# Moving operand addresses against the next stationary operand in a two-block transformer kernel

## The chip, the cores and the metric

One core of one Trainium2 chip runs the whole program. The metric is device time in microseconds from the first to the last instruction of the execution, with what lies around it; lower is better. Nothing is shared with other cores.

## The reference, cut to what matters

Two transformer blocks work on a sequence of 512 tokens of width 1024; the first of their three layers has a context of 256 tokens beside it. Between attention-like mixers stand six feed-forward networks, and these are most of the arithmetic:

```python
def swiglu(h, wi, wo):
    a, u = jnp.split(h @ wi, 2, axis=-1)      # 1024 -> 2 x 2816
    return (jax.nn.silu(a) * u) @ wo          # 2816 -> 1024
x = x + 0.5 * m[2] * swiglu(modulate(x, norm_g[l, 0], m[0], m[1]), ffn1_wi[l], ffn1_wo[l])
```

The modulation vectors `m` are products of a conditioning vector with large matrices, which the kernel reads while the feed-forward networks run.

## The kernel before, in words

Activations lie transposed: eight tiles `x0` to `x7` of 128 features by 512 tokens. Every float32 operand of a large product is split into a rounded part and a remainder, both of type float32r, so that `mm3` does three matmuls for one product: high weights by high activations (L182), high weights by low activations (L183), low weights by high activations (L184). The weights (`whi`, `wlo`, 128 columns of 512 bytes) are stationary, the activations (`hx`, `hc`, `g`, `mixr`, `mixa`: 512 or 256 columns) move through. TensorE therefore loads a new stationary operand ahead of every matmul, 16,678 times.

A feed-forward network (`ffn`, numbered 0 to 5) runs in four parts of 5, 5, 6 and 6 blocks of 128 hidden features. In each block `up` does 48 matmuls of the tiles `hx0` to `hx7` into `pau` (and 48 of `hc0` to `hc7` into `pc` in ffn 0, which has the context), `gate` makes a tile `g`, and at the end of a part `down` multiplies the `g` tiles into `py`, for eight output tiles `d`. The last four `d` of the last part, the tail, run by halves of 256 columns, so that the norm that follows can begin. A network that follows another begins with its first two blocks by halves too (256 columns), with weights that were fetched early into a pool `wb` by `prefetch` (two blocks' weights, or one block's in ffn 1 and 3). The mixers between use `fm` (weights stationary, activations moving) and `tm` (L668 to L670: activations stationary, 256 columns of weights moving).

Weights come by DMA on SyncE's queue into `wraw`, ScalarE makes `whi` (L177) and VectorE `wlo` (L178). The Tile framework orders the instructions by the waits that the tiles need; a tile may take over memory when the last reader of what lay there is done.

Where a tile lies follows from the order in which pools are opened and tiles first used. Pools on the left are stacked upward: constants, the `x` tiles, the weight pool `wp`, the temporaries `tp`, and above them the pools of the stage, among them `g0` to `g5` with the tiles `g`. Pools on the right are stacked downward from the end of the partition: `top` (a pad of 32 bytes), `hp0` with `hx0` to `hx7`, then `hc` and, when open, `wb`. A tile begins at a multiple of 32 bytes. The built program of the kernel before lists these first bytes of a partition:

| operand | first byte of one of its tiles | modulo 256 |
|---|---|---|
| `whi`, `wlo` in `wp` | 53056, 69440 | 64 |
| `hx`, also as `mixr` and `ph` | 196544 | 192 |
| `hc` | 180128 | 160 |
| `g` of ffn 0, tokens and context | 123264, 149888 | 128 |
| `g` of ffn 1, 3, 4, 5 | 102656 | 0 |
| `g` of ffn 2 | 124224 | 64 |
| `mixa` of the first, of the second mixer | 143424, 132864 | 64, 0 |
| weights in `wb` for ffn 1 to 5 and `w_in_2` | 163776 | 192 |
| weights in `wb` for `w_in` | 163712 | 128 |

The halves, the low parts, the blocks within a weight tile and the further tiles of a kind lie whole multiples of 256 bytes further on.

Of the kernel before, what the change touches and what calls it, by code (L numbers as in the profile page):

```python
# [8 lines left out]
F32 = mybir.dt.float32  # L9
F32R = mybir.dt.float32r  # L10
# [7 lines left out]
KC = 8  # L18
# [9 lines left out]
COLS = {}  # L28
NCST = 0
for _name, _w in [("b0", 72), ("b1", 72), ("b2", 72), ("ng0", 24), ("ng1", 24), ("fg", 8), ("pscale", 8),  # L30
                  ("gf1", 8), ("gmx", 8), ("gf2", 8), ("gfin", 8), ("gmh", 4), ("ba", 4), ("gbias", 1), ("glag", 1),
                  ("edge", 64),
                  ("gqk", 2)]:
    COLS[_name] = (NCST, NCST + _w)
    NCST += _w
CM = {n: 128 * i for i, n in enumerate(["ident", "glaf", "glab", "wprev", "wnext", "trif", "trib"])}
# [3 lines left out]
def program(ctx: ExitStack, tc: tile.TileContext, A, out):  # L40
    nc = tc.nc
    V, S, G, PE = nc.vector, nc.scalar, nc.gpsimd, nc.tensor
    const = ctx.enter_context(tc.tile_pool(name="const", bufs=1))
    act = ctx.enter_context(tc.tile_pool(name="act", bufs=1))
    wp = ctx.enter_context(tc.tile_pool(name="wp", bufs=2))
    tp = ctx.enter_context(tc.tile_pool(name="tp", bufs=2))
    pools = {}

    def opened(name, **kw):
        kw.setdefault("bufs", 1)  # L50
        g = tc.tile_pool(name=name, reuse_waits="tile", **kw)
        pools[name] = (g, g.__enter__())
        return pools[name][1]

    def opened_psum(name):
        return opened(name, bufs=2, space=bass.MemoryType.PSUM)

    def closed(*names):
        for name in names:
            pools.pop(name)[0].__exit__(None, None, None)  # L60
# [2 lines left out]
        for name in list(pools)[::-1]:  # L63
            closed(name)

    cst = const.tile([128, NCST], F32, name="cst")

    def C(name, i0=0, n=None):
        a, b = COLS[name]
        return cst[:, a + i0:(a + i0 + n) if n else b]  # L70
# [3 lines left out]
    ident = const.tile([128, 128], F32, name="ident")  # L74

    def load_constants():
        nc.sync.dma_start(cst, A["cst"])
        nc.sync.dma_start(ident, A["cmat"][:, CM["ident"]:CM["ident"] + 128])

    epst = const.tile([128, 4], F32, name="epst")  # L80
# [9 lines left out]
    def tmp(shape, dt=F32, name="tmp"):  # L90
        return tp.tile([128] + shape, dt, name=name, tag="t2k", bufs=5)
# [60 lines left out]
    def load_raw(src, shape):  # L152
        raw = wp.tile([128] + shape, F32, name="wraw", tag="raw", bufs=4)
        nc.sync.dma_start(raw, src)
        return raw

    def load_w(src, shape):
        return split_w(load_raw(src, shape), shape)

    ready = []  # L160

# [4 lines left out]

    def prefetched():
        if "wb" in pools:
            closed("wb")

    def take(src, shape):
        return ready.pop(0) if ready else load_w(src, shape)

    def split_w(raw, shape, pool=None, i=""):
        hi = (pool or wp).tile([128] + shape, F32R, name="whi", tag=f"whi{i}", bufs=1 if pool else 4)
        lo = (pool or wp).tile([128] + shape, F32R, name="wlo", tag=f"wlo{i}", bufs=1 if pool else 4)
        S.activation(hi, raw, AF.Copy)  # L177
        V.tensor_tensor(lo, raw, hi.bitcast(F32), OP.subtract)  # L178
        return hi, lo
# [6 lines left out]
    def split(src, hi, lo):  # L186
        a = S.activation(hi, src, AF.Copy)  # L187
        return a, V.tensor_tensor(lo, src, hi.bitcast(F32), OP.subtract)  # L188
# [78 lines left out]
    def new_h(s, pool):  # L267
        return [pool.tile([128, 2, s.n], F32R, name=f"h{s.name}{d}", tag=f"h{s.name}{d}", bufs=1) for d in range(KC)]
# [62 lines left out]
    def ffn(n, streams, hs, gate_m, steps, norm, early=None, g2=None, start=None, fused=False, nxt=(), mid=None, lag=False):  # L331
        X = streams[0]
        cx = streams[1] if len(streams) > 1 else None
        gp = opened(f"g{n}")
        ada_pool[0] = gp
        psum = opened_psum(f"pf{n}")
        gts = {}

# [14 lines left out]

        def gate(s, f, o):
            sl = tmp([s.n], name="sl")
            g = gp.tile([128, 2, s.n], F32R, name="g", tag=f"g{s.name}", bufs=6 if cx else 7)
            S.activation(sl, o[0], AF.Silu)  # L357
            V.tensor_tensor(sl, sl, o[1], OP.mult)  # L358
            gts[s.name, f] = g
            return split(sl, g[:, 0, :], g[:, 1, :])  # L360

        def wi(f):
            return [load_w(A[f"wi{n}"][f, p], [4, 2, 128]) for p in range(2)]

        def down(s, py, hi, lo, fs, c0, c1):
            for i, f in enumerate(fs):
                g = gts[s.name, f]
                mm3(py[:, :c1 - c0], hi[:, i, :], lo[:, i, :], g[:, 0, c0:c1], g[:, 1, c0:c1], i == 0, i == len(fs) - 1)

        def resid(s, d, py, c0, c1, last):  # L370
            V.scalar_tensor_tensor(s.x[d][:, c0:c1], py[:, :c1 - c0], s.gate[:, d:d + 1], s.x[d][:, c0:c1],  # L371
                                   op0=OP.mult, op1=OP.add)
            if last:
                s.square(d, c0, c1, g2)

        for pi, (f0, f1) in enumerate(PARTS):
            nk = f1 - f0
# [3 lines left out]
            if pi == 0:  # L381
                o = {f: bank2(X) for f in (0, 1)}
                if start:
                    o[2] = [psum.tile([128, T], F32, name="pau", tag="y") for _ in range(2)]
                    w, raw = {f: [] for f in range(3)}, {}
# [15 lines left out]
                else:  # L401
                    w = {f: [take(A[f"wi{n}"][f, p], [4, 2, 128]) for p in range(2)] for f in (0, 1)}
# [7 lines left out]
                    for f in (0, 1):  # L410
                        up(X, w[f], o[f], range(KC), *X.halves[1])
                    todo = todo[2:]
                    prefetched()
                for f in o:
                    last_gate = gate(X, f, o[f])
# [21 lines left out]
            def downs(ss, ds):  # L437
                for d in ds:
                    hi, lo = load_w(A[f"wo{n}_{pi}"][d], [nk, 128])
                    for s in ss:  # L440
                        py = psum.tile([128, 512], F32, name="py", tag="y")
                        down(s, py, hi, lo, fs, 0, s.n)
                        resid(s, d, py, 0, s.n, last)
# [17 lines left out]
            nt = 4 if last else 0  # L461
# [4 lines left out]
                if last and nxt[d:d + 1]:  # L466
                    prefetch(nxt[d:d + 1])
            if last:
                w = [load_w(A[f"wo{n}_{pi}"][KC - nt + i], [nk, 128]) for i in range(nt)]
                half = {s.name: norm(s) for s in streams}  # L470
                tail = [(s, c0, c1) for s in streams[::-1] for c0, c1 in s.halves]
                for s, c0, c1 in tail:
                    for i in range(nt):
                        py = psum.tile([128, 512], F32, name="py", tag="y")
                        down(s, py, w[i][0], w[i][1], fs, c0, c1)
                        resid(s, KC - nt + i, py, c0, c1, True)
                    if lag and c0:
                        late.apply()
                    late = Late(s, c0, c1, fused, half[s.name])
                    if (s, c0) != tail[-1][:2]:  # L480
                        late.sums(psum.tile([128, 512], F32, name="stat", tag="m"))
                        late.spread(not lag)
# [4 lines left out]
        closed(f"pf{n}", f"g{n}")  # L487

    xs = [act.tile([128, T], F32, name=f"x{d}") for d in range(KC)]
    opened("top", side="right").tile([128, 8], F32, name="pad", tag="pad")  # L490
    hpool = opened("hp0", side="right")
    hcpool = opened("hc", side="right")
    hcpool.tile([128, 8], F32, name="pad", tag="pad0")
    adp = opened("ad", side="right")
    cpool = opened("cp")
    cs = [cpool.tile([128, TC], F32, name=f"c{d}") for d in range(KC)]
# [1 line left out]
    CX = Stream("c", cs, "cc", cpool)  # L498

    h0 = {"x": new_h(X, hpool), "c": new_h(CX, hcpool)}  # L500
    hcpool.tile([128, 8], F32, name="pad", tag="pad1")
    gs0 = tp.tile([128, 8], F32, name="gs", tag="gs", bufs=4)
    raws, rx = {}, {}

# [149 lines left out]
    def win(name, i, m=256):  # L654
        return [load_w(A[name][i, p], [4, m]) for p in range(2)]
# [32 lines left out]
    w = [take(None, None) for p in range(2)]  # L688
# [19 lines left out]
    w = win("w_in", 6)  # L708
    for p in range(2):
        evac(qb[p], fm(pj(), w, hx, p, 0, T), scale=0.125)  # L710
    w = win("w_in", 0)
# [218 lines left out]
    for i in range(2):  # L930
        w = win("w_in", 1 + i)
# [153 lines left out]
    plp = opened("pool")  # L1085
    HP = 16 + T + 8
    hp = [plp.tile([128, HP], F32, name=f"hp{d}") for d in range(KC)]
    carry = plp.tile([128, 2 * KC], F32, name="carry")[:, 0:KC]
    for d in range(KC):
        G.memset(hp[d][:, 0:16], 0.0)  # L1090
        G.memset(hp[d][:, 16 + T:HP], 0.0)
# [26 lines left out]
    def pool_out(t0, t1, d, s):  # L1118
        win_ = WINS[d // 2]
        hw = win_ // 2  # L1120
        e = C("edge", 16 * (d // 2), 16)
        if t0 == 0:
            V.tensor_tensor(s[:, 8:8 + hw], s[:, 8:8 + hw], e[:, 0:hw], OP.mult)
        elif hw > 1:
            z = 8 + T - t0
            V.tensor_tensor(s[:, z - hw + 1:z], s[:, z - hw + 1:z], e[:, 8:8 + hw - 1], OP.mult)
        sv = s[:, 8:8 + t1 - t0]
        V.scalar_tensor_tensor(sv, sv, 1.0 / win_, hp[d][:, 16 + t0:16 + t1], op0=OP.mult, op1=OP.subtract)
        hi = ph[d][:, 0, t0:t1]
        S.activation(hi, sv, AF.Copy)  # L1130
        eng = V if (t0 and d < 4) or (not t0 and d > 5) else G
        eng.tensor_tensor(ph[d][:, 1, t0:t1], sv, hi.bitcast(F32), OP.subtract)
# [93 lines left out]
    gqk = tmp([2, 16], name="gqk")  # L1226
# [26 lines left out]
    w = [take(None, None) for p in range(2)]  # L1253
# [60 lines left out]
    for hf in range(2):  # L1314
        w = win("w_in_2", 8 + hf)
# [216 lines left out]
    for n in range(16):  # L1532
        hp, i = divmod(n, 4)
# [183 lines left out]
```

## Time and profile before

| | |
|---|---|
| median of three runs | 3190.74 us (3184.74 to 3191.72) |
| the profiled execution | 3192.12 us, its span 3190.3 us |
| mean granted TensorE clock | 0.985 of full speed |
| TensorE busy | 3074.2 us, 96% of the span |
| VectorE, ScalarE, GpSimd busy | 1764.8, 1144.0, 272.8 us |
| bytes read from HBM | 376.76 MB, 119 GB/s over the span |

The profiled execution is 1.4 us above the median of the runs, and 1.8 us of it lie outside the span. In a group of instructions the busy time is the union of their durations. Matmuls are pipelined: the duration of one is modelled and longer than the interval to the next, so the pace of TensorE is read as a length of time divided by the matmuls that began in it.

### The profile page before, as it was taken

The numbers are of one execution on the slowest core, as the hardware profiler recorded it, in microseconds if no ns is written. First come the engines' busy times: TensorE is split into PE (matmuls) and PEld (weight loads), VectorE is DVE, ScalarE is ACT, GpSimd is POOL, SyncE is SP. The second block draws the span as 40 slices with busy tenths as digits, with TensorE's granted clock in tenths as the row PEclk, the third lists the DMA queues.
The fourth block names the chain that finished last, engine by engine and source line by source line (L and its number), as shares of the span: only waits on it lengthen the run. The fifth ranks groups of instructions, "written<-read, shape, count | busy, mean of one in ns | idle before, by whom it ended". The sixth has DMA issues, their size and how long they took to land.

```text
span 3190.3 us, 41925 instructions
## 1 busy us (share of the span) xinstructions
PE 3074.2 (96%) x16678; PEld 2585.4 (81%) x16678; DVE 1764.8 (55%) x2952; ACT 1144.0 (36%) x1904; POOL 272.8 (9%) x263
## 2 busy tenths in 40 slices
PE   6899999999899999999997999999999999999998
PEld 4788888888678888888886888888888898788887
DVE  8875535535765555655457545555533557843334
ACT  4532212433543222522234322253223556632222
POOL 4300000211100000100003000010000221110000
PEclk8999999999999999999998999999999999999999
DMA  5653525111113454445451345534433221112331
GB/s 218 240 185 105 172 90 162 56 57 54 47 41 107 157 175 162 128 156 165 145 192 47 123 155 171 174 109 147 159 99 109 78 67 54 59 58 92 107 99 62
DMA packets 118040, 381.59 MB, mean 120 GB/s; under 512 B 13490, under 2 KB 17458, under 8 KB 117844
## 3 DMA queue, kind: packets, MB, share of 16 engines
q1 hardware_dynamic: 117844, 378.91, 36.7%
q8 instruction: 131, 2.15, 0.3%
q14 instruction: 65, 0.53, 0.1%
HBM read 376.76 MB, written 2.10 MB: 119 GB/s over the span
## 4 chain that ended last, share of the span: by engine, by line
PE 86%; DVE 8%; ACT 3%; issue 2%; POOL 1%; DMA 1%; DVEq 0%; ACTq 0%; POOLq 0%; SPq 0%
PE pau L183 15%; PE pau L184 15%; PE pau L182 15%; PE py L182 8%; PE py L183 8%; PE py L184 8%; PE pj L668 1%; PE pj L669 1%; PE pj L670 1%; PE pj L183 1%; PE pj L182 1%; PE pc L182 1%; PE pc L183 1%; PE pc L184 1%; PE pj L184 1%
## 5 line engine op out<-in xcount | busy, mean ns | idle before, releaser
L182 PE MATMUL pau<-hx,whi 128*128 128x512 f32 (+1 forms) x2272 | 864.9, 382 | 22.3 <-ACT hx L187 10.7
L183 PE MATMUL pau<-hx,whi 128*128 128x512 f32 (+1 forms) x2272 | 868.3, 382 | 6.5 <-DVE hx L188 4.4
L184 PE MATMUL pau<-hx,wlo 128*128 128x512 f32 (+1 forms) x2272 | 867.1, 382 | 0.0
L177 ACT ACTIVATE whi<-wraw 128x1024 fp32r<-128x1024 f32 (+2 forms) x538 | 510.2, 954 | 930.7 <-PE py L183 446.7
L178 DVE TENSOR_TENSOR wlo<-wraw,whi 128x1024 fp32r<-128x1024 f32 (+2 forms) x538 | 591.0, 1103 | 320.4 <-ACT whi L177 311.2
L182 PEld LDWEIGHTS pau<-hx,whi 128*128 128x128 f32 x2272 | 432.7, 191 | 110.8 <-ACT hx L187 12.0
L183 PEld LDWEIGHTS pau<-hx,whi 128*128 128x128 f32 x2272 | 433.5, 191 | 96.0 <-DVE hx L188 6.7
L184 PEld LDWEIGHTS pau<-hx,wlo 128*128 128x128 f32 x2272 | 433.4, 191 | 87.7 <-DVE wlo L178 0.4
L182 PE MATMUL py<-g,whi 128*128 128x512 f32 (+1 forms) x1376 | 492.1, 358 | 9.2 <-DVE x L371 7.1
L183 PE MATMUL py<-g,whi 128*128 128x512 f32 (+1 forms) x1376 | 489.2, 356 | 1.1 <-DVE g L188 1.1
L184 PE MATMUL py<-g,wlo 128*128 128x512 f32 (+1 forms) x1376 | 488.6, 355 | 0.0
L124 DVE CUSTOM_DVE_ANT_0 junk<-adaw,cv_c,cst 128x1024 bf16<-128x1024 f32 x192 | 246.5, 1284 | 204.5 <-DMA adaw<-in_ada 203.3
L371 DVE SCALAR_TENSOR_TENSOR x<-py,gate,x 128x512 f32<-128x512 f32 (+1 forms) x216 | 149.0, 690 | 290.3 <-PE py L184 289.4
L182 PEld LDWEIGHTS py<-g,whi 128*128 128x128 f32 x1376 | 259.2, 188 | 53.1 <-ACT hc L281 5.7
L183 PEld LDWEIGHTS py<-g,whi 128*128 128x128 f32 x1376 | 259.4, 189 | 41.2 <-DVE g L188 1.4
L184 PEld LDWEIGHTS py<-g,wlo 128*128 128x128 f32 x1376 | 259.1, 188 | 40.5
L357 ACT ACTIVATE sl<-pau 128x512 f32<-128x512 f32 x132 | 78.9, 598 | 519.0 <-PE pau L184 518.8
L358 DVE TENSOR_TENSOR sl<-sl,pau 128x512 f32<-128x512 f32 x132 | 90.7, 687 | 298.5 <-PE pau L184 279.4
L216 POOL TENSOR_TENSOR acc<-acc,sq 128x512 f32<-128x512 f32 (+1 forms) x33 | 43.1, 1309 | 2309.5 <-ACT sq L214 2309.3
L187 ACT ACTIVATE g<-sl 128x512 fp32r<-128x512 f32 (+1 forms) x154 | 92.4, 601 | 112.6 <-DVE sl L358 110.6
L668 PE MATMUL pj<-whi,hx 128*128 128x256 f32 x448 | 129.3, 289 | 0.3 <-ACT vtok L675 0.3
L669 PE MATMUL pj<-whi,hx 128*128 128x256 f32 x448 | 126.5, 282 | 0.0
(417 smaller groups left out, 3630.6 us busy)
## 6 DMA issues: line engine op xcount, KB each, us to landing
wraw<-in_wi SPq DMA_DIRECT2D x274, 512.0 KB, 3.4
adaw<-in_ada SPq DMA_DIRECT2D x192, 512.0 KB, 3.8
wraw<-in_wo SPq DMA_DIRECT2D x96, 384.0 KB, 3.1
wraw<-in_wo SPq DMA_DIRECT2D x104, 320.0 KB, 3.0
wraw<-in_w_in SPq DMA_DIRECT2D x42, 512.0 KB, 3.4
adas<-in_ada SPq DMA_DIRECT2D x32, 512.0 KB, 6.2
wraw<-in_w_out SPq DMA_DIRECT2D x16, 512.0 KB, 3.4
wraw<-in_ada SPq DMA_DIRECT2D x8, 512.0 KB, 4.1
```

The lines of the kernel that those rows point to most:

```text
L124: V.tensor_tensor_reduce(junk, raw, cvec(vec), 1.0, C(f"b{l}", c, 1), OP.mult, OP.add, mods[dst][:, c:c + 1])
L177: S.activation(hi, raw, AF.Copy)
L178: V.tensor_tensor(lo, raw, hi.bitcast(F32), OP.subtract)
L182: PE.matmul(o, wh, xh, start=start, stop=False)
L183: PE.matmul(o, wh, xl, start=False, stop=False)
L184: return PE.matmul(o, wl, xh, start=False, stop=stop)
L187: a = S.activation(hi, src, AF.Copy)
L357: S.activation(sl, o[0], AF.Silu)
L358: V.tensor_tensor(sl, sl, o[1], OP.mult)
L371: V.scalar_tensor_tensor(s.x[d][:, c0:c1], py[:, :c1 - c0], s.gate[:, d:d + 1], s.x[d][:, c0:c1], op0=OP.mult, op1=OP.add)
L668: PE.matmul(o, xh, hi[:, k % 4, :], start=k == 0, stop=False)
L669: PE.matmul(o, xl, hi[:, k % 4, :], start=False, stop=False)
```

## The change

It moves operands by a few bytes, so that the first byte of a moving operand less the first byte of the stationary operand that is loaded next is 0 modulo 256 for 512 columns and 192 modulo 256 for 256 columns, in most places. The pad in `top` grows from 32 to 160 bytes, the pads around `hc` change, the pools of `g` get a pad of 64 or 192 bytes (none in ffn 2), the context's `g` a further one of 192, the pool `wb` one of 192 at its end, and the tail's weights begin 64 bytes into their buffers. To have room for this the table `edge` (256 bytes of each partition) leaves the constants and is loaded by a DMA of its own into the pool of the pooling mixer, on SyncE's queue ahead of ffn 2. No matmul is added, removed or reordered by the text of the kernel.

```diff
-                  ("edge", 64),
-                  ("gqk", 2)]:
+                  ("gqk", 2), ("edge", 64)]:
...
-    cst = const.tile([128, NCST], F32, name="cst")
+    cst = const.tile([128, COLS["edge"][0]], F32, name="cst")
...
-        nc.sync.dma_start(cst, A["cst"])
+        nc.sync.dma_start(cst, A["cst"][:, :COLS["edge"][0]])
...
-    def load_w(src, shape):
-        return split_w(load_raw(src, shape), shape)
+    def load_w(src, shape, shift=0):
+        return split_w(load_raw(src, shape), shape, shift=shift)
...
         if "wb" in pools:
+            pools["wb"][1].tile([128, 48], F32, name="pad", tag="pad", bufs=1)
             closed("wb")
...
-    def split_w(raw, shape, pool=None, i=""):
-        hi = (pool or wp).tile([128] + shape, F32R, name="whi", tag=f"whi{i}", bufs=1 if pool else 4)
-        lo = (pool or wp).tile([128] + shape, F32R, name="wlo", tag=f"wlo{i}", bufs=1 if pool else 4)
+    def split_w(raw, shape, pool=None, i="", shift=0):
+        if shift:
+            n = shape[0] * shape[1]
+            hi, lo = [wp.tile([128, n + shift], F32R, name=nm, tag=nm, bufs=4)[:, shift:]
+                      .rearrange("p (a b) -> p a b", a=shape[0]) for nm in ("whi", "wlo")]
+        else:
+            hi = (pool or wp).tile([128] + shape, F32R, name="whi", tag=f"whi{i}", bufs=1 if pool else 4)
+            lo = (pool or wp).tile([128] + shape, F32R, name="wlo", tag=f"wlo{i}", bufs=1 if pool else 4)
...
         ada_pool[0] = gp
+        if n != 2:
+            gp.tile([128, 16 if n else 48], F32, name="pad", tag="pad")
...
             sl = tmp([s.n], name="sl")
+            if s.name == "c" and f == 0:
+                gp.tile([128, 48], F32, name="pad", tag="padc")
...
-                w = [load_w(A[f"wo{n}_{pi}"][KC - nt + i], [nk, 128]) for i in range(nt)]
+                w = [load_w(A[f"wo{n}_{pi}"][KC - nt + i], [nk, 128], 16) for i in range(nt)]
...
-    opened("top", side="right").tile([128, 8], F32, name="pad", tag="pad")
+    opened("top", side="right").tile([128, 40], F32, name="pad", tag="pad")
     hpool = opened("hp0", side="right")
     hcpool = opened("hc", side="right")
-    hcpool.tile([128, 8], F32, name="pad", tag="pad0")
...
     h0 = {"x": new_h(X, hpool), "c": new_h(CX, hcpool)}
-    hcpool.tile([128, 8], F32, name="pad", tag="pad1")
+    hcpool.tile([128, 16], F32, name="pad", tag="pad1")
...
     carry = plp.tile([128, 2 * KC], F32, name="carry")[:, 0:KC]
+    edge = plp.tile([128, 64], F32, name="edge")
+    nc.sync.dma_start(edge, A["cst"][:, COLS["edge"][0]:])
...
-        e = C("edge", 16 * (d // 2), 16)
+        e = edge[:, 16 * (d // 2):16 * (d // 2) + 16]
```

## Rows read from the trace of the kernel before

**Rows 1.** The page: busy time by engine, and the chain that ended last.
```profile
PE 3074.2 (96%) x16678; PEld 2585.4 (81%) x16678; DVE 1764.8 (55%) x2952; ACT 1144.0 (36%) x1904; POOL 272.8 (9%) x263
...
PE 86%; DVE 8%; ACT 3%; issue 2%; POOL 1%; DMA 1%; DVEq 0%; ACTq 0%; POOLq 0%; SPq 0%
```

**Rows 2.** Busy time in stretches: length, PE, PEld, DVE, ACT, POOL; clock, DMA share, GB/s.
```profile
0.00:110.00 110.00, 80.79 (x264) 58.55 (x265) 90.17 (x113) 49.43 (x76) 44.14 (x23) 0.89 0.63 228
...
1325.00:1706.00 381.00, 379.97 (x1854) 317.88 (x1852) 206.89 (x292) 124.31 (x180) 18.41 (x34) 1.00 0.46 148
1706.00:1745.00 39.00, 21.81 (x80) 17.28 (x80) 33.69 (x76) 19.10 (x43) 17.03 (x20) 0.69 0.07 27
```

**Rows 3.** TensorE's groups by line and shape: count, busy us, mean ns, idle before.
```profile
L182 PE MATMUL pau<-hx,whi 128*128 128x512 f32 x1952 | 771.7, 397 | 15.9 <-ACT hx L187 10.7 <-ACT hx L281 5.2
L182 PE MATMUL py<-g,whi 128*128 128x512 f32 x912 | 360.0, 395 | 7.1 <-DVE x L371 5.3 <-DVE mod_cc L516 1.8
L182 PE MATMUL py<-g,whi 128*128 128x256 f32 x464 | 132.1, 285 | 2.1 <-DVE x L371 1.8
L668 PE MATMUL pj<-whi,hx 128*128 128x256 f32 x448 | 129.3, 289 | 0.3 <-ACT vtok L675 0.3
L182 PE MATMUL pc<-hc,whi 128*128 128x256 f32 x352 | 99.1, 281 | 1.9 <-DVE sl L358 1.9
L182 PE MATMUL pau<-hx,whi 128*128 128x256 f32 x320 | 93.3, 291 | 6.4 <-ACT hx L281 3.9 <-ACT sq L214 1.4 <-DVE x L1045 1.0
```

**Rows 4.** Stretches, matmuls into `py` alone: length, PE busy (count), clock, DMA share, GB/s.
```profile
1198.60:1232.20 33.60, 33.60 (x144) 1.00 0.40 126
1569.81:1602.46 32.65, 32.65 (x144) 1.00 0.41 129
3143.19:3159.98 16.79, 16.79 (x72) 1.00 0.08 24
296.02:299.45 3.43, 3.43 (x17) 1.00 0.20 45
597.87:608.45 10.58, 10.58 (x91) 1.00 0.22 74
1685.99:1694.60 8.61, 8.61 (x73) 1.00 0.25 84
2485.93:2494.08 8.15, 8.15 (x73) 1.00 0.23 76
```

**Rows 5.** Stretches, matmuls into `pau` alone.
```profile
1131.67:1198.60 66.93, 66.93 (x288) 1.00 0.55 175
1419.41:1475.40 55.99, 55.99 (x240) 1.00 0.52 165
1341.35:1358.69 17.34, 17.34 (x144) 1.00 0.37 122
24.00:110.00 86.00, 69.56 (x240) 0.86 0.56 200
```

**Rows 6.** A stretch, matmuls into `mb` alone (`hx` moving).
```profile
2525.36:2530.15 4.79, 4.79 (x21) 1.00 0.02 3
```

**Rows 7.** A stretch, matmuls of `mixa` alone.
```profile
934.49:945.41 10.92, 10.92 (x48) 1.00 0.30 96
```

**Rows 8.** A stretch, matmuls into `pc` alone.
```profile
207.01:212.76 5.75, 5.75 (x48) 1.00 0.39 120
```

**Rows 9.** Stretches, matmuls into `pj` alone.
```profile
645.53:650.97 5.44, 5.43 (x48) 1.00 0.00 0
2543.94:2566.81 22.87, 22.87 (x192) 1.00 0.31 93
```

**Rows 10.** Timeline of SyncE's queue around the end of ffn 1: start, length.
```profile
1318.18 0.90 SPq L95 DMA_DIRECT2D cv_c<-in_c  x2
1350.49 1.46 SPq L141 DMA_DIRECT2D adaw<-in_ada  x2
```

**Rows 11.** Timeline of GpSimd there: start, length, idle before and its releaser.
```profile
1334.43 0.11 POOL L1090 MEMSET hp<- 128x16 f32 x1 [0.83 <-PE py L184]
```

## The prediction, on record before the result

> **What bounds the kernel now.** I read the page's busy times and chain first. TensorE is busy 96% of the span and 86% of the chain that ended last is its own matmuls [rows 1]: the reader is to see that little else counts. The stretches say where that holds. From 1325 to 1706 us (ffn 2, and the other networks look like it) TensorE is busy for 379.97 of 381.00 us, while VectorE has 54% and the DMA engines 46% of that time [rows 2]. Only the first 110 us and the pooling mixer (1706 to 1745 us) have it idle for long: 80.79 of 110.00 and 21.81 of 39.00 us [rows 2]. So the end is set by how many matmuls there are and how far apart they start. A duration in the groups (397 ns for 512 columns [rows 3]) is no pace, because the next matmul starts before that end; I therefore took stretches that hold one kind of matmul, from its first start to the next kind's, and divided length by count.
>
> The pace differs where instructions look alike. `py<-g` with 512 columns takes 33.60/144 = 233.3 ns in ffn 1, 32.65/144 = 226.7 ns in ffn 2, and 16.79/72 = 233.2 ns in ffn 5 [rows 4]. Line, shape, engine and granted clock (1.00, the 2.4 GHz level) agree. DMA traffic is not the difference: its share is 0.40, 0.41 and 0.08 [rows 4]. What differs is where `g` lies: by the table of first bytes, moving less next stationary is 0-64 = 192 modulo 256 in ffn 1 and 5, and 64-64 = 0 in ffn 2. I sorted the other stretches by this residue.
>
> 512 columns: residue 128 (`hx` into `pau`) takes 66.93/288 = 232.4 and 55.99/240 = 233.3 ns [rows 5], mean 232.8; residue 64 (`g` in ffn 0) 3.43/15 = 228.7, since 2 of the 17 counted had begun before [rows 4]; residue 0 also 10.92/48 = 227.5 with `mixa` [rows 7] and 4.79/21 = 228.1 with `hx` itself, from early-fetched weights [rows 6], which is 0.03 us over 21 times 226.8 for settling after a switch. 256 columns: residue 0 takes 17.34/144 = 120.4 (mostly; `hx` halves [rows 5]) and 8.61/72 = 119.6 ns (tail of ffn 2 [rows 4]); 96 takes 5.75/48 = 119.8 (`hc` [rows 8]); 128 takes 22.87/192 = 119.1 (`tm` [rows 9]); 64 takes 10.58/90 = 117.6 in one place [rows 4] and 5.44/48 = 113.3 in another [rows 9]; 192 takes 8.15/72 = 113.2 [rows 4]. (In the tails one counted matmul had begun before.)
>
> **The change part by part.** The left stack loses 256 bytes, so residues there stay. `hx` moves down 128 bytes: its residue with `wp` weights goes from 128 to 0. `g` gains 64 bytes in ffn 1, 3, 4, 5 (192 to 0) and 192 in ffn 0 (64 to 0); the context's `g` gains 384 (64 to 192). `hc` moves down 160 (96 to 192), weights in `wb` 320 (`hx` halves: 0 to 192). The tail's weights move up 64 (token halves end at 192).
>
> The terms, each a count times a difference of two paces:
> - `hx` into `pau`, 512 columns: three lines of 1952 are 5856 [rows 3]. 240 of them stand in the start stretch, where TensorE is busy only 69.56 of 86.00 us [rows 5]; there VectorE's and DMA's work covers the gain, worth 1.4 us if that cover were gone, and I take 0. The other 5616 gain 232.8-226.8 = 6.0 ns: 33.7 us.
> - `g`, 512 columns: 912 per line, 456 per network [rows 3]. ffn 1, 3, 4, 5: 1824 times 233.3-226.8 = 6.5 ns, 11.9 us; ffn 0: 456 times about 2 ns, 0.9 us; ffn 2: nothing.
> - `hx` and `mixr` in the mixers, 432 of 512 columns by the loops: 2.6 us; I take 2, since a mixer's TensorE waits more.
> - `hc` into `pc`: 1056 [rows 3] times 119.8-113.3 = 6.5 ns, 6.9 us.
> - `g`, 256 columns: about 600 of ffn 0 from 117.6 to 113.3, 2.6 us; 144 of ffn 2's tail from 119.6, 0.9 us.
> - `hx` halves with `wb` weights: 768 of the 960 [rows 3] times 120.4-113.3 = 7.1 ns, 5.5 us. They start while VectorE and ScalarE still make `hx` (6.4 us of waits in this group [rows 3]), and what they gain may be waited away: 0 to 5.5, I take 2.7.
> - Losses: `tm`, 3 times 448 and some [rows 3], goes from 128 to 0, about 1 ns each on 1440, 1.3 us; the tail of the context, `hx` halves with `wp` weights, `ph` and `mb` lose some 1.0 us together.
> - Settling after a switch of kind (0.03 us [rows 6], some 90 switches): 2.7 us lost.
>
> Sum: 33.7 + 11.9 + 0.9 + 2 + 6.9 + 3.5 + 2.7 - 2.3 - 2.7 = 56.6, say 57 us.
>
> The new `edge` DMA (32 KB) costs nothing by its place. Its bytes lie over a `g` tile of ffn 1, so it waits as the memset of `hp` does, until 1334.43 us [rows 11]. Behind it on SyncE may stand the loads of `cv_c` (1318.18) and the modulation rows, which now go at 1350.49 [rows 10]. `cv_c` would go 16 us later and still before the first row that needs it; beyond 1350.49 each us of delay would reach TensorE one for one through ffn 2's weights, and 57 us more would be needed to undo the gain. The shorter load of constants and the bigger pads cost no instruction. After the gain the next to be late is VectorE, far off at 54% in a network [rows 2].
>
> The rows show that a matmul's pace goes with the address of what is loaded meanwhile [rows 4]. The Trainium skill says the opposite: in "TensorE: Matmul & The Clock Gate", section "Step-by-step: what each phase is for", TensorE has two independent read ports, and loading the next weights takes no read bandwidth from the running matmul; in "SBUF — State Buffer", section "Who interferes with whom", TensorE waits on nobody. By that rule the sum would be 0 us instead of 57. This trace does not agree: 226.7 against 233.3 ns.
>
> **Bounds.** Small end: `hx` settles only to 228.1 [rows 6], (232.8-228.1) times 5616 = 26.4 us; `g` to 228.1, 9.5; `hc` to 117.6 [rows 4], 2.3; 256-column `g` of ffn 2 0.3; early halves and mixers 0; losses 2.3: 36 us. Large end: `hx` from 233.3, 36.5; start 1.4; mixers 2.6; `g` 12.8; `hc` 6.9; `g` halves 3.5; early halves 5.5; losses 2.3, no settling: 67 us.
>
> **The rivals.**
> - `hx` keeps its pace: what is seen at residue 0 belongs to `g` and `mixa`, and of `hx` only 21 matmuls speak for the gain [rows 6]. Then 35.7 of the 57 us fall away: 21 us, 3169. Against it: these 21 are the same tile, line and shape.
> - Placement decides nothing and 226.7 has another cause, say what ran before ffn 2: 3190.7. For it stands only that ffn 2 alone has the quick `py`; against it `mixa` in another place [rows 7] and the 256-column pairs. The two independent ports of the Trainium skill's "TensorE: Matmul & The Clock Gate" ("Step-by-step: what each phase is for") would give the same.
> - Slower: the sign turns on `hx`, because its 5616 pairs come in another order (two blocks read the same `hx` in turn, while `g` changes every third matmul). If each lost 6.6 ns as `g` gains it, that is 37 us against the other 23 us gained: 3205. It decides from 4.1 ns per pair. Rows 6 speak against it: 228.1 is below 232.8.
>
> **How the numbers follow.** The sum is made against the profiled execution: 3192.1 - 57 = 3135 us; the median of the runs is 1.4 us lower, 3190.7 - 57 = 3134 us, and that is the forecast. Chances: forecast 0.85, `hx` unmoved 0.07, nothing 0.05, slower 0.03. From the bounds the forecast's own range is 3124 to 3155; I give 3122 to 3158, which holds nearly all of it and no rival, about 0.82. Within 0.2% (6.4 us) is what a measurement of this kernel can hardly tell from no change. Faster 0.92, same 0.05, slower 0.03.
>
> **What would show it.** Right: `py<-g` of ffn 1 at 27.2 us per 120 and `pau<-hx` at 65.3 us per 288 matmuls with TensorE still busy all through; `pc` at 5.4 us per 48; `tm` no quicker; the first 110 us and the pooling mixer as long as before; SyncE's next load after `edge` not later than now. Wrong: `pau<-hx` still at 232 ns or above, TensorE idle in the networks for weights or gates, or another order of the instructions at ffn 2's begin.

## The result and the profile after

The changed kernel takes 3139.82 us (median of four runs, 3138.73 to 3140.43); the kernel before, run beside it, 3187.90 (3184.74 to 3191.72). The ratio is 0.9848 [0.9831, 0.9865]: 48 us less, or 51 against the median shown ahead of the prediction. The forecast was 3134, its range 3122 to 3158. For 512 columns the mechanism held; the gain came out about 6 us smaller than the sum, and the terms for 256 columns are where it fell short.

The page of the changed kernel, busy times and the chain that ended last, to be held against [rows 1]. Its line numbers are some lines higher than before's: `mm3` is L187 to L189.
```profile
PE 3023.7 (96%) x16678; PEld 2580.1 (82%) x16678; DVE 1763.7 (56%) x2952; ACT 1142.1 (36%) x1904; POOL 273.8 (9%) x263
...
PE 86%; DVE 8%; ACT 3%; issue 2%; DMA 1%; POOL 1%; DVEq 0%; SPq 0%; ACTq 0%; POOLq 0%
```
As many matmuls as before occupy TensorE for 50.5 us less, VectorE's and ScalarE's work is within 2 us of what it was, and the chain has the same shares. So the time went out of the matmuls themselves and no other engine became the bound.

The stretches that answer to [rows 2], the start, ffn 2 and the pooling mixer (same columns):
```profile
0.00:110.00 110.00, 80.30 (x266) 58.57 (x267) 90.13 (x113) 49.54 (x76) 44.52 (x23) 0.88 0.64 227
1307.00:1681.00 374.00, 372.75 (x1859) 316.71 (x1858) 206.63 (x293) 123.84 (x180) 18.53 (x34) 1.00 0.48 154
1681.00:1720.00 39.00, 21.86 (x80) 17.37 (x80) 33.82 (x75) 18.99 (x42) 17.19 (x20) 0.69 0.08 27
```
ffn 2 takes 374 us instead of 381, with TensorE still busy all through; the start and the pooling mixer are what they were.

Stretches of the changed kernel, matmuls into `py` alone, against [rows 4]: 512 columns in ffn 1 (two parts), ffn 2 and ffn 5, then the tails of ffn 1 and ffn 4 by 256 columns.
```profile
1009.92:1037.12 27.20, 27.20 (x120) 1.00 0.46 149
1184.00:1216.64 32.64, 32.64 (x144) 1.00 0.41 128
1547.10:1579.74 32.64, 32.64 (x144) 1.00 0.41 130
3091.73:3108.04 16.31, 16.31 (x72) 1.00 0.09 25
1298.24:1306.70 8.46, 8.46 (x73) 1.00 0.25 84
2442.31:2450.77 8.46, 8.46 (x73) 1.00 0.25 81
```
27.20/120, 32.64/144 and 16.31/72 are 226.5 to 226.7 ns: ffn 1 and ffn 5 (233.3 and 233.2 before) now run as ffn 2 always did. The tails are the surprise: these two rows are the first 256-column halves of the tails of ffn 1 and ffn 4, their residue was 192 before and is 192 now, and they went from 113.2 [rows 4] to 8.46/72 = 117.5 ns.

The same for `pau` [rows 5], the last two of them early halves (256 columns) of ffn 2 and ffn 4; then `pc` [rows 8] and `mb` [rows 6].
```profile
1118.72:1184.00 65.28, 65.28 (x288) 1.00 0.56 181
1400.22:1454.62 54.40, 54.40 (x240) 1.00 0.54 170
1323.94:1340.35 16.41, 16.41 (x144) 1.00 0.37 116
2101.21:2118.24 17.03, 17.03 (x144) 1.00 0.34 118
```
```profile
207.06:212.71 5.65, 5.65 (x48) 1.00 0.48 161
```
```profile
2480.24:2485.12 4.88, 4.88 (x21) 1.00 0.02 3
```
`hx` with 512 columns runs at 65.28/288 = 226.7 ns, to the tenth what the prediction named (65.3 us per 288). `pc` does not: 5.65/48 = 117.7 ns, where 5.4 us per 48 were named. The early halves come out at 114.0 ns in ffn 2 and 118.3 in ffn 4, at one residue, 192. `mb`, which the change moved from residue 0 to 192, lost 0.09 us: 4.88/21 = 232.4 ns. It reads the same `hx` tiles that `pau` reads, at the same place, with weights at another place; so in one kernel one moving address has both paces, and it is the distance between the two operands that goes with the pace, not the moving address alone.

SyncE's queue of the changed kernel at the end of ffn 1, against [rows 10]:
```profile
1315.45 0.33 SPq L1098 DMA_DIRECT2D edge<-in_cst  x1
1315.83 0.90 SPq L94 DMA_DIRECT2D cv_c<-in_c  x2
1333.24 1.46 SPq L140 DMA_DIRECT2D adaw<-in_ada  x2
```
The new DMA goes at 1315.45 us, `cv_c` right behind it, and the modulation rows 17.8 us after it, 17 us earlier in the span than before.

TensorE executes its matmuls in the same order in both kernels. So each matmul's interval to the next (start to start) can be subtracted from the same one's in the other trace. By kind, in us, beside the forecast:

| term | forecast | traces |
|---|---|---|
| `pau<-hx`, 512 columns, 5616 | 33.7 | 33.3 |
| the same in the start stretch, 240 | 0 | 0.6 |
| `py<-g`, 512 columns, 2736 | 12.8 | 12.6 |
| `hx` and `mixr` in the mixers, 512 columns | 2.0 | 1.6 |
| `pc<-hc`, 256 columns, 1056 | 6.9 | 0.4 |
| `py<-g`, 256 columns | 3.5 | 1.0 |
| `pau<-hx`, 256 columns (early halves) | 2.7 | 3.3 |
| `tm` | -1.3 | -3.2 |
| other losses and settling; in the traces all else | -3.7 | 2.1 |
| sum | 56.6 | 51.7 |

The right column holds more than paces: where TensorE waited, or where the granted clock stood at its lower level in one trace and not at the same place of the other, that is in it too. The part on why the prediction came out as it did takes it apart.

### The profile page after: what moved, and what is told of

The parts are those of the page before. It is cut to its first block, busy times and chain, and to the rows that moved or that the text cites. A ratio compares the mean times of both kernels' runs of the same rounds, so it can differ in the third digit from the quotient of the medians.

```text
span 3138.6 us, 41926 instructions
## 1 busy us (share of the span) xinstructions
PE 3023.7 (96%) x16678; PEld 2580.1 (82%) x16678; DVE 1763.7 (56%) x2952; ACT 1142.1 (36%) x1904; POOL 273.8 (9%) x263
## 4 chain that ended last, share of the span: by engine, by line
PE 86%; DVE 8%; ACT 3%; issue 2%; DMA 1%; POOL 1%; DVEq 0%; SPq 0%; ACTq 0%; POOLq 0%
PE pau L188 15%; PE pau L189 15%; PE pau L187 15%; PE py L187 8%; PE py L188 8%; PE py L189 7%; PE pj L188 1%; PE pj L189 1%; PE pj L187 1%; PE pj L676 1%; PE pj L677 1%; PE pj L678 1%; PE pc L187 1%; PE pc L189 1%; PE pc L188 1%
## 5 line engine op out<-in xcount | busy, mean ns | idle before, releaser
L187 PE MATMUL pau<-hx,whi 128*128 128x512 f32 (+1 forms) x2272 | 853.3, 377 | 23.3 <-ACT hx L192 11.7
L188 PE MATMUL pau<-hx,whi 128*128 128x512 f32 (+1 forms) x2272 | 855.6, 377 | 6.0 <-DVE hx L193 3.8
L189 PE MATMUL pau<-hx,wlo 128*128 128x512 f32 (+1 forms) x2272 | 854.2, 376 | 0.0
L187 PEld LDWEIGHTS pau<-hx,whi 128*128 128x128 f32 x2272 | 430.5, 190 | 101.7 <-ACT hx L192 12.9
L187 PE MATMUL py<-g,whi 128*128 128x512 f32 (+1 forms) x1376 | 488.3, 355 | 8.9 <-DVE x L380 6.2
L189 PEld LDWEIGHTS pau<-hx,wlo 128*128 128x128 f32 x2272 | 430.7, 190 | 77.2 <-DVE wlo L183 0.4
L189 PE MATMUL py<-g,wlo 128*128 128x512 f32 (+1 forms) x1376 | 485.2, 353 | 0.0
L187 PEld LDWEIGHTS py<-g,whi 128*128 128x128 f32 x1376 | 258.9, 188 | 48.2 <-ACT hc L286 5.1
L189 PEld LDWEIGHTS py<-g,wlo 128*128 128x128 f32 x1376 | 259.1, 188 | 35.6
```

Of the source, the lines that this page charges most:

```text
L187: PE.matmul(o, wh, xh, start=start, stop=False)
L188: PE.matmul(o, wh, xl, start=False, stop=False)
L189: return PE.matmul(o, wl, xh, start=False, stop=stop)
```

## The experiments

Two questions stood. Is it the address difference that sets the pace, for `hx` as for `g`? And why did 256 columns at residue 192 not give 113.3 ns?

**A sweep of residues (two runs of matmuls per residue).** The kernel leaves the whole computation out and runs only matmuls on two buffers, in the access pattern of `mm3`, 72 per residue, once with rising and once with falling residues; then 256 columns behind runs of 512 of a chosen residue; then operands that alternate by 128 bytes, so that the residue to the own and to the next stationary operand differ.
```diff
+        for i in range(count):
+            k, part = divmod(i, 3)
+            k %= 4
+            w = W[:, (2048 if part == 2 else 0) + 128 * k:][:, :128]
+            e = 1024 * k + 512 * (part == 1) + r // 4
+            PE.matmul(o[:, :n], w, X[:, e:e + n], start=i == 0, stop=i == count - 1)
```


> This kernel leaves out the whole computation: it copies x to the output and runs matmuls on two buffers, 72 of them for each residue of moving less next stationary (0, 4, 8, then steps of 16 bytes modulo 256), for 512 and for 256 columns, once in rising (u) and once in falling order (d). If the residue sets the pace, 512 columns take 226.7 ns at 0, about 229 at 64, about 233 at 128 and 192, in both orders; if the pace of before came from what else ran in ffn 2, all residues agree within 1 ns. Then the stationary operands alternate by 128 bytes: with 0 to the operand in use and 128 to the next, the theory of the next operand says about 233 ns, a theory of the operand in use 226.7; with 128 to the operand in use and 0 to the next it is the other way round. Last, 96 matmuls of 256 columns at 192 and at 64 follow 24 of 512 columns at 0, 64, 128 and 192: if the pace of 256 columns is a phase that is inherited from the matmuls before, 192 takes 117.8 ns behind 512 at 0 and 113.3 behind 512 at 192; if the address alone sets it, all four are equal.

Stretches of the sweep, one residue each, 512 columns at residues 0, 4, 128, 192 and 240:
```profile
39.57:55.89 16.32, 16.32 (x72) 1.00 0.00 0
55.89:73.04 17.15, 17.15 (x72) 1.00 0.01 1
206.37:223.11 16.74, 16.74 (x72) 1.00 0.00 1
273.41:290.21 16.80, 16.80 (x72) 1.00 0.00 0
323.90:340.23 16.33, 16.33 (x72) 1.00 0.00 1
```
That is 226.7, 238.2, 232.5, 233.3 and 226.8 ns: with no VectorE work and a DMA share of 0.00 to 0.01, the pace goes with the residue, and 0, 128 and 192 give what the kernels gave there. All others lay at 228.9 to 234.7. So a residue of 0 modulo 256 (or 240) is the quick one, and 4 bytes beside it is the slowest. Not every residue has one pace, though: at 48, 176 and 208 the rising and the falling pass differ, at 208 most, by 16.90/72 against 16.56/72, 234.7 against 230.0 ns:
```profile
290.21:307.11 16.90, 16.90 (x72) 1.00 0.00 1
```
```profile
526.38:542.94 16.56, 16.56 (x72) 1.00 0.00 1
```

256 columns gave a first hint of what went wrong. At 112 both passes settled at 113.3 ns, at 0 both at 119.8 to 120. At 192 the rising pass gave 117.8 and the falling one 113.8. Behind 24 matmuls of 512 columns it was steered; residue 192 behind residues 0 and 192, then 64 behind 0 and 64, 96 matmuls each:
```profile
952.69:964.00 11.31, 11.31 (x96) 1.00 0.01 1
...
1002.88:1013.76 10.88, 10.88 (x96) 1.00 0.01 2
...
1019.22:1030.53 11.31, 11.31 (x96) 1.00 0.01 1
...
1036.03:1046.91 10.88, 10.88 (x96) 1.00 0.01 2
```
That is 117.8 or 113.3 ns by what ran before, and it stayed for all 96. Residue 192 was quick behind 128 and 192 and slow behind 0 and 64; residue 64 was quick behind 64 alone.

The alternating pair was to say which stationary operand counts. With the own at 0 and the next at 128 it took 22.72/96 = 236.7 ns, with the own at 128 and the next at 0 22.08/96 = 230.0. The direction speaks for the next operand; neither figure is the pace at residue 0 or at 128, so the addresses of more than one pair enter, and how is open. Nearly everywhere else in these runs the own and the next stationary operand lie a multiple of 256 bytes apart, so they cannot be told from each other; that it is the next one that counts is not shown.

**`hx` alone.** Of the change only the pads ahead of and behind `hx` and `hc`, and the `edge` table, are kept: `hx` comes to residue 0, `hc` and `g` stay.
```diff
...
-    opened("top", side="right").tile([128, 8], F32, name="pad", tag="pad")
+    opened("top", side="right").tile([128, 40], F32, name="pad", tag="pad")
...
-    hcpool.tile([128, 8], F32, name="pad", tag="pad1")
+    hcpool.tile([128, 40], F32, name="pad", tag="pad1")
```


> Of the change only the room (edge moved out of the constants) and the 128 bytes under hx; hc, g, the early-fetched and the tail's weights keep their residues. Residue theory: the 5616 matmuls of hx with 512 columns that TensorE is bound by go from 232.8 to 226.7 ns, 34 us, less 1.5 us for tm and the halves with wp weights at 0: 32 to 33 us faster, about 3155 us; py of ffn 1 stays at 233.3 ns and pc at 119.8. Rival (the gain needs all the operands moved together, or comes from the changed waits around the edge table): under 10 us, or a gain that shows in py and pc too.

Measured: 3156.41 us (3155.51 to 3156.75) against 3188.81, ratio 0.9900 [0.9885, 0.9914], 32.4 us less. In its trace the `pau` stretch of ffn 1 runs at 226.7 ns. The second of these rows, the tail of ffn 1, was no part of the edit:
```profile
1223.47:1288.77 65.30, 65.30 (x288) 1.00 0.61 199
```
```profile
1305.57:1313.74 8.17, 8.17 (x73) 1.00 0.22 81
```
The rival of a gain that needs all the operands moved together falls with the time, and that of a gain from the changed waits with the operands that stayed: `py` of ffn 1 keeps 33.60/144 = 233.3 ns,
```profile
1189.87:1223.47 33.60, 33.60 (x144) 1.00 0.40 131
```
and `pc` keeps 120 ns. The first half of the tail, too, still takes 8.17/72 = 113.5 ns at residue 192, behind `g` with 512 columns at residue 192. In the changed kernel it has the same residue, stands behind `g` at residue 0 and takes 117.5. The sweep showed the same at 192 behind 192 and behind 0.

**`g` alone.** Only the pad ahead of the `g` tiles and the `edge` table are kept.
```diff
...
+        if n != 2:
+            gp.tile([128, 16 if n else 48], F32, name="pad", tag="pad")
```


> Of the change only the room and the pads in the pools of g (64 bytes, 192 in ffn 0); the context's g goes with the others to residue 0, and the tail's weights are not shifted, so the tails of ffn 1, 3, 4, 5 go from 192 to 0 with 256 columns. Residue theory: py with 512 columns goes from 233.3 to 226.7 ns in ffn 1, 3, 4 and 5 and from 228.7 in ffn 0 (12.8 us gained), the halves lose 576 times 6.5 ns at most and the context 600 times 2 ns (4.9 us lost): 8 to 11 us faster, about 3178 us; pau stays at 232.4 to 233.3 ns. Rival (hx and g gain only together): no gain beyond 3 us.

Measured: 3178.92 us (3174.37 to 3179.45) against 3188.81, ratio 0.9968 [0.9954, 0.9982], 9.9 us less. In ffn 1 `py` comes to 32.66/144 = 226.8 ns and `pau` stays at 66.96/288 = 232.5:
```profile
1195.70:1228.36 32.66, 32.66 (x144) 1.00 0.39 130
```
```profile
1228.36:1295.32 66.96, 66.96 (x288) 1.00 0.60 199
```

**The 256-column places alone.** `hx` with 512 columns and the tokens' `g` keep their places; `hc`, the context's `g` and the early halves come to residue 192.
```diff
...
+            pools["wb"][1].tile([128, 48], F32, name="pad", tag="pad", bufs=1)
...
+                gp.tile([128, 32], F32, name="pad", tag="padc")
...
-    hcpool.tile([128, 8], F32, name="pad", tag="pad1")
+    hcpool.tile([128, 48], F32, name="pad", tag="pad1")
```


> Of the change only what concerns 256 columns: hc from 96 to 192, the early-fetched weights (hx halves from 0 to 192), the context's g from 64 to 192; hx and g of the tokens keep 128, 192 and 64. Inherited pace: behind hx at 128 the runs of pc go from 119.8 to 113.3 ns, 6.9 us, with 0 to 5.5 us from the early halves: 7 to 12 us faster, 3177 to 3182 us, more than the 5 or 6 us that are left of the whole change once hx (32 us) and g (10 us) alone are taken off it. Address alone: pc takes 117.8 as in the changed kernel, 2 us, 2 to 7 us in all.

Measured: 3181.70 us (3177.38 to 3182.65) against 3189.39, ratio 0.9976 [0.9967, 0.9985], 7.7 us less. By the interval that is 5 to 10 us, which overlaps both forecasts, so the time does not decide between them. The trace shows more. Stretches of `pau` (512 columns, residue 128) and of the `pc` right behind each (residue 192):
```profile
194.31:205.45 11.14, 11.14 (x48) 1.00 0.73 242
320.04:331.23 11.19, 11.19 (x48) 1.00 0.62 208
336.67:347.87 11.20, 11.20 (x48) 1.00 0.57 189
```
```profile
205.45:211.11 5.66, 5.66 (x48) 1.00 0.45 141
331.23:336.67 5.44, 5.44 (x48) 1.00 0.37 137
347.87:353.31 5.44, 5.44 (x48) 1.00 0.28 96
```
The `hc` tiles keep one place and the weights one residue, and `pc` takes 5.66/48 = 117.9 ns in the first case and 5.44/48 = 113.3 in the others, for all six blocks between 320 and 420 us. The `pau` in between has two paces as well, 232.1 and 233.1 to 233.3 ns, which go along. The other sixteen blocks take 117.8 or 117.9, although they too stand behind residue 128, where the sweep had 192 quick. So 113.3 ns at residue 192 is no property of the residue, nor of the pair of residues; it is one of two paces that persist from block to block. What turned those six blocks to it the runs do not say.

The three parts alone give 32.4 + 9.9 + 7.7 = 50.0 us, and the whole 48 to 53 (the second measurement below included).

**256 columns behind residue 0.** Again no computation but the matmuls: 48 of 512 columns at residue 0, then 48 of 256 at one of sixteen residues, and the whole list three times.
```diff
+    for n in range(3):
+        for r in range(0, 256, 16):
+            run(f"p{n}to{r}", 512, 0, 48)
+            run(f"c{r}round{n}", 256, r, 48)
```


> Leaves out the whole computation like the first sweep. Runs of 48 matmuls of 512 columns at residue 0 and of 48 with 256 columns at each residue in steps of 16 alternate, three rounds, as in the body of ffn 0 of the changed kernel. If the pace of 256 columns is inherited where more than one is possible, 192 and 64 take 117.8 ns in all three rounds, never 113.3; a residue that has only the quick pace (112 had it in both orders of the first sweep) takes 113.3 here too. If it is a matter of chance, the rounds differ from one another. 512 columns take 226.7 ns throughout.

All three rounds agree to 0.1 ns. Residue 112, then 192, in the first:
```profile
167.06:172.54 5.48, 5.48 (x48) 1.00 0.01 3
```
```profile
249.81:255.46 5.65, 5.65 (x48) 1.00 0.00 0
```
That is 114.2 and 117.7 ns. The other fourteen residues lay between 116.7 and 120.1, with 0, 80, 96 and 128 slowest. Behind 512-column matmuls at residue 0, then, 192 gives 117.8 each time when nothing interrupts, which is the pace of the changed kernel's `pc` and of the first halves of its tails.

**The tail at 112.** The changed kernel with the tail's weights 36 columns into their buffers instead of 16, which puts the tail at residue 112.
```diff
-                w = [load_w(A[f"wo{n}_{pi}"][KC - nt + i], [nk, 128], 16) for i in range(nt)]
+                w = [load_w(A[f"wo{n}_{pi}"][KC - nt + i], [nk, 128], 36) for i in range(nt)]
```


> The changed kernel with the tail's weights 144 instead of 64 bytes into their buffers, so that the halves of g stand at 112 instead of 192 (the context's tail at 48). If 112 has only the quick pace, as in both sweeps, the tails run at 113.3 to 114.2 instead of 117.8 ns: 838 matmuls, at most 3.1 us, of which the second halves may wait some away: 1.5 to 3 us faster than the changed kernel, 3137 to 3139 us. If the pace of 256 columns in the kernel has another cause than in the sweeps, they stay at 117.8 and the time at 3140.

A miss: 3140.20 us (3136.25 to 3141.84), ratio 0.9846 [0.9831, 0.9861], and the tail of ffn 1 became slower, 8.63/72 = 119.9 ns:
```profile
1296.53:1305.16 8.63, 8.63 (x73) 1.00 0.23 80
```

**The same with `hc` at 112**, reached by the moving side: the `hc` tiles begin 16 bytes further into one large tile.
```diff
...
+        if s.name == "c":
+            whole = pool.tile([128, 4 + KC * 512], F32R, name="hc", tag="hc", bufs=1)
+            return [whole[:, 4 + 512 * d:516 + 512 * d].rearrange("p (a b) -> p a b", a=2) for d in range(KC)]
...
-    hcpool.tile([128, 16], F32, name="pad", tag="pad1")
+    hcpool.tile([128, 32], F32, name="pad", tag="pad1")
```


> The same, and the eight tiles hc in one tile that begins 16 bytes further in, so that pc runs at 112 instead of 192 as well. pc behind pau at 226.7 goes from 117.8 to about 114.2 ns over a run of 48 (the second sweep's mean with its settling): 1056 times 3.6 ns, 3.8 us more, 3133 to 3136 us. If one tile for all of hc brings waits, pc or pau shows idle time before it, and the gain is smaller or turns.

Measured: 3135.98 us (3134.91 to 3137.79), ratio 0.9835 [0.9821, 0.9849]; `pc` at 114.1 ns per matmul, the tails again at 119.8. One residue, two outcomes; the two places differ in which operand had been moved, which the run after next tries by itself.

**The changed kernel once more**, on the same chip as these two.


> The changed kernel once more, beside the two that follow: 3139 to 3141 us.

3137.71 us (3136.61 to 3140.52), ratio 0.9840 [0.9827, 0.9853], 52.9 us less, and a little quicker than expected. The two traces of the changed kernel, one program with the same addresses and the same order, differ in the first 240 matmuls of `pc`, where TensorE waits on the way. The last 96 of them, in the first trace and in this one:
```profile
170.43:181.74 11.31, 11.31 (x98) 1.00 0.42 117
```
```profile
167.79:178.67 10.88, 10.88 (x98) 1.00 0.48 144
```
Two of the 98 counted had begun before, so that is 11.31/96 = 117.8 and 10.88/96 = 113.3 ns. Up to a wait (2.5 us long in the first trace, 1.0 us in this one) both ran at 117.8. Addresses and order, then, do not fix which of the two paces a run gets. The traces differ in the length of that wait and in a stretch of lower clock behind it in the first one (164.7 to 167.9 us); which of these decides is open.

**Which side is moved.** Matmuls alone: 72 of 256 columns behind 48 of 512 at residue 0, the residue made by the moving operand (`m`), by the stationary one (`s`), or by that with the moving tiles taken downward (`d`), twice over.
```diff
+            w = W[:, (2048 if part == 2 else 0) + 128 * k + (-s // 4) % 64:][:, :128]
+            e = 1024 * (3 - k if down else k) + 512 * (part == 1) + (r - s) // 4
```


> Leaves out the whole computation. 72 matmuls of 256 columns behind 48 of 512 columns at residue 0, at 16, 48, 64, 112 and 192, the residue made by the moving operand (m), by the stationary one (s, as in the tails), or by the stationary one with the moving tiles walked downward (d, as the tails of ffn 1 do); twice. If the residue and the matmuls before are all that counts, m, s and d agree, and 112 takes 113.3 ns in each. If the side that is shifted counts, s at 112 takes the 119.8 ns of the tails at 112 and m the 114.2 of pc.

Residue 112 by the moving, then by the stationary side:
```profile
224.83:233.03 8.20, 8.20 (x72) 1.00 0.01 2
```
```profile
243.94:252.57 8.63, 8.63 (x72) 1.00 0.01 2
```
113.9 and 119.9 ns, the same in both rounds and for `d`. At 16 and 48 the side counts too (118.7 against 117.3, 118.4 against 116.7); at 64 and 192 all three forms give 117.8. So at the residues tried that are odd multiples of 16 bytes the difference alone doesn't fix the pace. That accounts for the miss of the tail.

**`hc` alone at 112**, on the changed kernel (the `hc` part of the diff above, the tail as in the change).


> The changed kernel with hc alone at 112 (one tile, 16 bytes further in), the tail's weights as in the change. pc at 114.1 instead of 117.8 ns as in the run before, 1056 times 3.7 ns, 3.9 us; the tails at 117.8 instead of the 119.8 that they had at 112: 3133 to 3136 us, ahead of the changed kernel (3137.7 and 3139.8 us). If one tile for hc costs waits, 3138 to 3140.

Measured: 3136.30 us (3134.69 to 3137.33) against 3188.90, ratio 0.9835 [0.9822, 0.9849]. A stretch of its `pc`:
```profile
205.73:211.22 5.49, 5.49 (x48) 1.00 0.44 135
```
5.49/48 = 114.4 ns where the changed kernel has 117.7. By the pace 3.3 ns times 1056, 3.5 us, could be had at most; the medians of the changed kernel are 1.4 and 3.5 us higher, on other chips, and the intervals of the ratios overlap. The pace is clear, a shorter time is not separable.

## Why the prediction came out as it did

**512 columns: right in mechanism and size.** The place of a moving operand against the stationary ones sets the pace, and at residue 0 every long run settled at 226.7 ns; that pace is now read for `hx` as for `g`, and the sweep gives it with nothing else running. That it is the next stationary operand, as the prediction has it, is the part that stays unproven. The terms for `hx`, `g` and the mixers came to 48.1 us of 48.5. The parts alone confirm the two large ones on the clock: 32.4 us for `hx`, 9.9 for `g`. The doubt that only 21 matmuls spoke for `hx` [rows 6] is settled, and with it the rival that `hx` keeps its pace, the one that nothing happens, and the slower one.

**256 columns: the term that was mis-sized.** The step said 113.3 ns at residue 192, from one stretch of 72 [rows 4], and the change was valued at 6.9 + 3.5 + 2.7 = 13.1 us. The traces give 0.4 + 1.0 + 3.3 = 4.7. Residue 192 has two lasting paces, 113.3 and 117.8 ns, and which one a run gets hangs on what went before. The row that the step used was a tail behind `g` at residue 192; the change moved that `g` to residue 0 and thereby took the quick pace away from the tails' first halves. The warning stood in [rows 4] and [rows 9]: residue 64 at 117.6 in one place and at 113.3 in another, which the prediction noted and priced as if it belonged to 64 alone. The small end of its bounds did take 117.6 for `hc`: 2.3 us, against 2.25 us in those of the 1056 intervals that are no waits. The other 1.9 us are no pace: 1.5 of them fell to the granted clock, which stood at the lower level (0.50, 1.2 GHz) in the trace of the changed kernel while `pc` ran,
```profile
164.70:167.90 3.20, 3.20 (x17) 0.50 0.67 224
```
and at 1.00 in the trace of the kernel before and in the second trace of the changed one; 0.4 went into a longer wait. Of the 1.0 us of `py`, 1.2 came from such a stretch of lower clock in the trace of the kernel before (at 623 us), 0.4 from shorter waits, and the intervals at full clock without a wait became 0.6 us longer: the first halves of the tails of ffn 1, 3, 4 and 5 lost 1.2 us, while ffn 2's tail and the first part of ffn 0 gained some 0.9.

**Early halves.** 2.7 us was a middle between 0 and 5.5, and 3.3 came, but only 2.4 of it by the pace (114.0 ns in ffn 2, 118.3 in ffn 4). Another 1.5 is a stretch of lower clock at the beginning of ffn 4 in the trace of the kernel before (at 2132 us), and longer waits took 0.6 back. So the size was hit partly by luck. What in ffn 4 turns it to the slower pace wasn't tried.

**Losses.** Settling was priced at 2.7 us and is mostly not there: in the changed kernel the 48 `pau` behind each `pc` run at 226.7 to 227.0 ns. It shows in short runs: `mixr`, moved to residue 0 too, gained nothing in its 142 intervals at full clock without a wait, since its runs of about ten matmuls between other kinds end before the pace is reached (234, 236, 224, 231, 235, 229, 232, 231, 227, 226 and 227 ns in one of the longest). `tm` was to lose 1.3 us; in intervals at full clock without a wait it lost 1.4. The rest of its 3.2 is clock and waiting: 3.1 us in intervals that one trace ran at the lower clock and the other did not, less 1.3 us of shorter waits. The larger of these clock events, the changed kernel at the start of `tm` in the last mixer, all of TensorE:
```profile
2496.00:2498.00 2.00, 0.25 (x2) 1.00 0.00 0
2498.00:2500.00 2.00, 2.00 (x12) 0.83 0.26 55
2500.00:2502.00 2.00, 2.00 (x12) 0.50 0.78 272
2502.00:2504.00 2.00, 2.00 (x16) 0.82 0.55 201
```
and the kernel before at the same place of the program:
```profile
2541.00:2543.00 2.00, 0.50 (x4) 1.00 0.00 0
2543.00:2545.00 2.00, 2.00 (x15) 1.00 0.24 41
2545.00:2547.00 2.00, 2.00 (x19) 1.00 0.83 268
2547.00:2549.00 2.00, 2.00 (x19) 1.00 0.58 219
```
In both TensorE was almost idle just before (0.25 and 0.50 of 2.00 us); in one the clock then fell to 1.2 GHz, in the other it stayed at 2.4. By the counts (12, 12 and 16 matmuls instead of 15, 19 and 19 in 2 us each) it cost some 13 matmuls' time, 1.6 us. The kernel with the tail at 112, whose `tm` has the same addresses, kept 1.00 there, so these addresses alone do not bring it; but the other four traces with the whole change show the fall at this place, and of the four without it none does. Whether the change brings it is open.

The total came closer than its terms. The three terms for 256 columns gave 8.4 us less than forecast and `tm` 1.9 less, and the row of losses and all else gave 5.8 more, since losses were priced that did not come and small gains elsewhere were not listed. That these offset each other is luck.

**`edge` and the start stretch.** The DMA cost nothing, as forecast: it went at 1315.45 us, the load that had to wait behind it went 17.8 us after it, and ffn 2 shows no new idle time. The start stretch gained 0.6 us of the 1.4 that were given as its bound.

**What one operand's load does to the other's.** The sweep, in which nothing but TensorE works, has 226.7 to 238.2 ns for 512 columns by the addresses alone. The Trainium skill's two independent read ports ("TensorE: Matmul & The Clock Gate", "Step-by-step: what each phase is for") would make these stretches alike; the runs do not agree. By which mechanism the two operands meet they do not say.

## What to carry to other kernels

Where a weight load runs beside each matmul and TensorE is busy all through, read the pace by stretch (from first start to first start, divided by the count), sort it by the address of the moving operand less that of the next stationary one modulo 256, and move pools by padding; with 512 float32r columns residue 0 was worth 6 ns in each of 8,000 matmuls. Before a pace is carried from one place to another, look whether two places with the same residue already differ: that is a state and not an address, and a change upstream can flip it. Measure such a pace in its place in the kernel and in more than one trace; a sweep gave the two paces but not always the one that the kernel took. Before a difference between two traces is put down to waits or to the change, look at the granted clock of the stretch in both.

## What the runs showed that I had not expected

- With 256 columns, residues 64 and 192 hold either 113.3 or 117.8 ns for at least 96 matmuls. In the sweep the matmuls before set which; in one kernel six blocks in turn ran at 113.3 and the blocks before and after them at 117.9 at the same residues, and one program took 117.8 in one execution and 113.3 in another for the same 96 matmuls.
- The side that is moved can matter: 113.9 against 119.9 ns at residue 112.
- With 512 columns, too, some residues have more than one pace (234.7 and 230.0 ns at 208); residue 0 settled at 226.7 in every long run, but after other matmuls only behind some eight of its own (the `mixr` intervals above).
- A moving operand 4 bytes off the best place is the slowest seen: 238.2 ns for 512 columns, 123 for 256. Residue 240 is as quick as 0 with 512 columns (226.8 ns), and one of the middle ones with 256 (117.2).
